# The head of a hybrid transformer block: modulation by blocks of 128 channels in TensorE column groups, against modulation by column halves

## The chip, the cores and the metric

The kernel runs on one core of a Trainium2 chip. The metric is the device time of one execution in microseconds (us), the median of several runs. Engines are named as in the profile: PE is TensorE's matmul side and PEld its weight loads, DVE is VectorE, ACT is ScalarE, POOL is GpSimd, and SP is SyncE, which here only issues DMA transfers (SPq is its row in the trace).

## The reference, cut to what matters

The kernel computes one layer of a trunk that carries a context stream `ctx` (256 tokens) and a latent stream `x` (1024 tokens) of 1024 channels through the same weights. The head is what the change is about:

```
mod   = silu(c)     @ w_mod + b_mod            # 1 x 6144
mod_c = silu(c_ctx) @ w_mod + b_mod
sh1, sc1, g1, sh2, sc2, g2 = split(mod, 6);  sh1c, sc1c, ... = split(mod_c, 6)
h  = x   * (1 + sc1)  + sh1
hc = ctx * (1 + sc1c) + sh1c
z    = h  @ w_in            # columns of four head groups: mLSTM, SGU, conv, S5
zc_d = hc @ w_in[:, OFF_D:] # the context goes into mLSTM and S5
...
x = layer_norm(ALPHA * x + g1 * (concat(y_a, y_b, y_c, y_d) @ w_out))
x = layer_norm(ALPHA * x + g2 * swiglu(x * (1 + sc2) + sh2))
```

The S5 group takes 256 columns of `z` for all 1280 tokens. Here they are computed as two products of 128 columns each, called block 0 and block 1 of the S5 input below.

## The kernel before, in words

Inputs of the large products are fp32 numbers split in a high and a low part (`hi`, `lo`), and a product is three passes: high by high, high by low, low by high (`PASSES`). `wload` fetches a weight tile of 512 KB into `raw`; `wsplit` makes its high part on ACT (L853, a CAST to `whl`) and its low part on DVE (L854). `projT` runs one such product with the channels as contraction, 8 steps `k` of 128 channels, into two PSUM banks of 512 latent tokens (L883) and one of 256 context tokens (L885). `projK` is the product with tokens as the output's partitions (L892).

A scheduler puts the instructions of the written program in an order for each engine, by data, by free buffers and by priority; each engine then runs its own list in that order and waits there by semaphores. So what the code writes first need not run first, but a queue is never overtaken once it is built. That holds for the list of SP too, whose transfers start in order.

The head, as it was written:

- `mod_load(cg)` fetches the part of `w_mod` that makes shift and scale, in two column groups `cg`: each is 4 pages of 1 MB (eight transfers of 512 KB), for 4 of the 8 channel blocks.
- `mod_cols(cg)` multiplies: `ccol` (both conditions after SiLU, 2 columns) is the stationary operand, 512 columns of `w_mod` stream by, for 8 steps `k` and two halves `j` (L820, 2 rows of output, fp32). Each of these 16 fp32 matmuls is two records in the trace. The two rows are copied out of PSUM (L824), turned into columns by 8 small transposes (L826), and with the bias added they go into `modc` (L830).
- `streams(ks)` applies scale and shift to four blocks of context (`vx`, L917) and latent (`xt`, `s5Yg`, `s5V`, `s5W`; L917 on DVE for odd blocks, L919 on ACT for even ones), casts to the high part on ACT (L920) and subtracts for the low part on DVE (L921).
- Then `projT` of S5 block 0 over the four channel blocks done; then the same again for column group 1. Block 1 comes later, in the loop over `b` behind the head, over all eight `k`.
- `s5_pre` and `s5_unit_tables` (on DVE, ACT and PE; lines L53 to L268) prepare the tables of the S5 recurrence; they depend on small parameters only and run between the other work.
- `zs` copies of ACT (L994) move the S5 input out of PSUM, a transfer writes it to `zd` in DRAM, and eight transfers for each block read it back as `s5U` with another layout. A table travels through DRAM in the same way: `s5TT` to `s5dr` to `s5M`. The units of the recurrence then start with PE's L287 on `s5U` and DVE's L292 on its result.

## Time and profile before

| | us |
|---|---|
| three runs before | 1180.8, 1176.69, 1179.63 |
| median | 1179.63 |
| the profiled execution, own time | 1178.48 |
| its span in the trace | 1176.70 |
| granted TensorE clock, mean | 0.986 |

The profiled execution is 1178.48 us by its own time, 1.78 us more than the span between its first and last record. Start times in the trace count from the span's start. A row of the timeline gives start, duration, engine, line of the kernel, operation, the tiles written and read, shape and the number of instructions put together in the row. Where a query puts several in a row, the duration is from the first's start to the last's end; matmuls overlap in it. A window row gives, for a stretch of time, its length, then the busy time of each engine with its instructions, the granted clock of TensorE (1.00 is full speed), the mean busy share of the 16 DMA engines and their rate in GB/s.

### The profile page before, as it was taken

The page shows a single profiled execution, that of the slowest core. Times are in us where ns is not written, and L with a number is a line of the kernel's source. Part 1 is how long each engine was busy: PE and PEld are TensorE (multiplying, and loading weights), DVE is VectorE, ACT ScalarE, POOL GpSimd, SP SyncE. Part 2 cuts the span into 40 slices and gives each one's busy share as a digit, 9 for nine tenths or more (in the row PEclk, how much of TensorE's full clock was granted, in tenths as well). Part 3 has the DMA queues.
Part 4 walks back from the last instruction along what each step waited for, and adds up shares of the span by engine and source line. Part 5 has one row for each costly group of instructions (what it writes and reads, how often), then busy time and mean ns, then how long its engine had stood idle before and what let it go on. Part 6 is the DMA issues. An engine that isn't in the chain of part 4 may idle for free.

```text
span 1176.7 us, 15244 instructions
## 1 busy us (share of the span) xinstructions
PE 1133.6 (96%) x5671; PEld 896.3 (76%) x5671; DVE 932.8 (79%) x1837; ACT 446.9 (38%) x691; POOL 9.6 (1%) x30
## 2 busy tenths in 40 slices
PE   6999999999999999989999999999999999999994
PEld 1487788667888778868887888888888878788883
DVE  6588999988899889879867667675767576777898
ACT  1454344422325433582233333233323243533433
POOL 0010000000000000000000000000000000000000
PEclk9999999999999999999999999999999989999997
DMA  9542111022143256352222233414342488856723
GB/s 362 208 128 88 45 48 49 35 68 72 54 143 109 90 170 207 106 217 84 96 106 102 80 125 125 139 44 141 107 143 82 134 291 281 290 197 212 268 70 143
DMA packets 57483, 160.57 MB, mean 136 GB/s; under 512 B 5377, under 2 KB 9633, under 8 KB 57026
## 3 DMA queue, kind: packets, MB, share of 16 engines
q1 hardware_dynamic: 56994, 158.62, 39.3%
q8 instruction: 44, 0.72, 0.2%
q0 software_dynamic: 272, 0.70, 0.2%
q10 hardware_dynamic: 144, 0.29, 0.1%
q14 instruction: 29, 0.24, 0.1%
HBM read 130.77 MB, written 28.82 MB: 136 GB/s over the span
## 4 chain that ended last, share of the span: by engine, by line
PE 77%; DVE 12%; DMA 7%; ACT 2%; issue 1%; POOL 0%; SPq 0%; DVEq 0%; ACTq 0%; POOLq 0%
PE mm L1344 16%; PE mm L883 13%; PE a L1344 8%; PE mm L1476 5%; PE mm L1183 5%; PE b L1344 4%; PE b L883 4%; PE a L1476 3%; PE b L1476 3%; PE mm L892 3%; DMA raw<-in_w_dram 2%; PE c L1476 2%; PE b L564 1%; DVE whl L854 1%; DMA whl<-gd 1%
## 5 line engine op out<-in xcount | busy, mean ns | idle before, releaser
L853 ACT CAST whl<-raw 128x512 fp32r<-128x512 f32 (+1 forms) x198 | 121.4, 622 | 278.6 <-PE mm L883 71.0
L883 PE MATMUL mm<-pg,whl 128*128 128x512 f32 x816 | 217.9, 406 | 1.4 <-ACT pg L1206 1.2
L1344 PE MATMUL mm<-pg,whl 128*128 128x512 f32 x864 | 204.8, 389 | 0.0
L1344 PEld LDWEIGHTS mm<-pg,whl 128*128 128x128 f32 x864 | 162.1, 188 | 33.8
L854 DVE TENSOR_TENSOR whl<-raw,whl 128x512 fp32r<-128x512 f32 (+1 forms) x198 | 135.5, 690 | 60.0 <-ACT whl L853 58.1
L883 PEld LDWEIGHTS mm<-pg,whl 128*128 128x128 f32 x816 | 147.6, 189 | 39.1 <-issue 7.0
L1344 PE MATMUL a<-pg,whl 128*128 128x512 f32 x432 | 104.2, 390 | 0.3 <-ACT whl L853 0.3
L1344 PEld LDWEIGHTS a<-pg,whl 128*128 128x128 f32 x432 | 80.9, 188 | 17.8 <-ACT whl L853 0.7
L1476 PE MATMUL mm<-pg,pg 128*128 128x512 f32 x315 | 88.2, 390 | 0.0
L853 ACT CAST pg<-raw 128x1024 fp32r<-128x1024 f32 (+1 forms) x46 | 45.7, 993 | 73.5 <-DVE raw L1455 38.7
L1476 PEld LDWEIGHTS mm<-pg,pg 128*128 128x128 f32 x315 | 59.0, 188 | 12.7 <-ACT pg L853 0.6
L854 DVE TENSOR_TENSOR pg<-raw,pg 128x1024 fp32r<-128x1024 f32 (+1 forms) x46 | 52.9, 1151 | 15.5 <-ACT pg L853 15.3
L892 PE MATMUL mm<-whl,pg 128*128 128x256 f32 (+1 forms) x448 | 63.1, 288 | 0.0
L892 PEld LDWEIGHTS mm<-whl,pg 128*128 128x128 f32 x448 | 58.1, 190 | 1.5 <-issue 1.1
L853 ACT CAST pg<-whl 128x1024 fp32r<-128x1024 f32 (+1 forms) x42 | 40.8, 976 | 38.8 <-DMA whl<-gd 19.3
L854 DVE TENSOR_TENSOR pg<-whl,pg 128x1024 fp32r<-128x1024 f32 (+1 forms) x42 | 47.3, 1131 | 8.3 <-ACT pg L853 8.1
L1344 PE MATMUL b<-pg,whl 128*128 128x512 f32 x216 | 51.9, 389 | 0.0
L1183 PE MATMUL mm<-whl,pg 128*128 128x512 f32 x192 | 50.2, 398 | 0.3 <-DVE pg L1171 0.3
L1183 PE MATMUL mm<-pg 128*128 128x512 f32 x192 | 49.4, 400 | 0.1
L1476 PE MATMUL a<-pg,pg 128*128 128x512 f32 x156 | 48.0, 389 | 0.0
L1476 PE MATMUL b<-pg,pg 128*128 128x512 f32 x156 | 48.0, 389 | 0.0
L1344 PEld LDWEIGHTS b<-pg,whl 128*128 128x128 f32 x216 | 40.5, 188 | 8.4
(473 smaller groups left out, 1796.9 us busy)
## 6 DMA issues: line engine op xcount, KB each, us to landing
raw<-in_w_dram SPq DMA_DIRECT2D x84, 512.0 KB
gd<-pg SPq DMA_DIRECT2D x22, 1024.0 KB
whl<-gd SPq DMA_DIRECT2D x35, 512.0 KB
pg<-in_wm_dram SPq DMA_DIRECT2D x16, 512.0 KB
raw<-in_wo_dram SPq DMA_DIRECT2D x16, 512.0 KB
raw<-in_wt_dram SPq DMA_DIRECT2D x14, 512.0 KB
mw<-in_w_mod_dram SPq DMA_DIRECT2D x24, 256.0 KB
vx<-in_w_mod_dram SPq DMA_DIRECT2D x24, 256.0 KB
```

What stands on the lines that cost most here:

```text
L564: pe.matmul(ps[:, x * 65:(x + 1) * 65], lhsT=D[d][:, x], rhs=vx[:, h, :], start=True, stop=True)
L853: a.copy(hi, r)
L854: v.tensor_tensor(lo, r, hi.bitcast(F32), op=SUB)
L883: pe.matmul(ps[h], lhsT=W(wi, k), rhs=rhs(hi, h, k), **f)
L892: pe.matmul(ps, lhsT=lhs(hi, k), rhs=Ws[k // 4](wi, k % 4), start=(k == 0 and n == 0), stop=(k == 7 and n == 2))
L1183: pe.matmul(ps, lhsT=Yr(hi, half, k)[:, t * 128:(t + 1) * 128], rhs=Ws[k // 2](wi, k % 2), start=(i + n == 0), stop=(i == 7 and n == 2))
L1344: pe.matmul(ps, lhsT=W[:, wi, k, :], rhs=B[b][hi][:, k], start=(first and k + n == 0), stop=(k == 3 and n == 2), skip_group_check=True)
L1476: pe.matmul(ps[t], lhsT=Ag[:, hi, k, t * 128:(t + 1) * 128], rhs=Bg[:, wi, k], start=(first and k0 + k + m == 0), stop=(k0 + k == NK - 1 a ...
```

## The change

Modulation and the first use of its result go by eight blocks of 128 channels.

- The host layout of `w_mod` is by block: `wm[k]` has, for one block, the 128 shift columns and the 128 scale columns over all 1024 contraction rows, 1 MB.
- `arrive(k)` fetches what block `k` needs: two halves of `wm[k]`, 512 KB of the latent, 128 KB of the context, and for the first two blocks the weight tile of S5 block `k`. The targets rotate in three (`s5Yg`, `vx`, and `s5h` with `s5V` for `wm`; three places of `xt` for the latent; `s5r1`, `s5r2`, `s5sc` for the context), so block `k+3` can be fetched once block `k` has been read.
- `modulate(k)` makes shift and scale of the block by 8 matmuls of 32 output rows and 256 columns (L903). The stationary operand `c32` has the two conditions in the first 2 of 32 columns and zeros in the others. Contraction steps `g` = 0 to 3 of a half go into four 32-row parts of one PSUM bank, which are four column groups of TensorE. One DVE copy takes 128x256 out of PSUM (L906), and two matmuls by a constant `quad` (L909) both sum the four parts and turn rows to columns. Two additions on DVE write `modc` (L911).
- The latent's scale is now on ACT for all blocks (L920), where odd blocks were on DVE.
- After `modulate(k)` the block goes through all three passes of both S5 products, into PSUM banks that both keep over the whole loop (`acc`); block 0 of the channels is used for S5 block 1 one step late. The `zs` copies of both S5 blocks stand behind channel block 7. `s5_pre` is written after the loop.

Line numbers in the head change: L820, L824, L826, L830 become L903, L906, L909, L911; L845, L853, L854 become L820, L828, L829; L883, L885, L892 become L858, L860, L867; L917, L919, L920, L921 become L918, L920, L921, L922. Behind the head a line of before is 8 lower, but L784 is L785.

```diff
-CST = (..., ("maskf", 128), ("maskb", 128))
+CST = (..., ("maskf", 128), ("maskb", 128), ("quad", 2))
...
-    g["wm"] = f(x["w_mod"][0][:, 0:2 * D].reshape(4, 2, 128, 2, 2, 512).transpose(4, 0, 2, 1, 3, 5))
+    g["wm"] = f(x["w_mod"][0][:, 0:2 * D].reshape(8, 128, 2, 8, 128).transpose(3, 1, 0, 2, 4))
...
+    c["quad"] = np.tile(np.eye(32, 2, dtype=np.float32), (4, 1))
...
-        def mod_cols(cg, ws, tags):
-        ...
-        def mod_load(cg):
-        ...
-        w0 = mod_load(0)
-        S = s5_pre(e, s5, A["s5p"])
-        ...
-        mod_cols(0, w0, "aa")
-        streams(range(4))
-        Wd[0] = wsplit(Wd[0])
-        zps = [projT(Wd[0], (0, 1), Hr, hcr, ks=range(4), last=False)]
-        mod_cols(1, w1_, "ac")
-        streams(range(4, 8))
+        c32 = s5.tile([128, 8, 32], F32, name="c32", tag="s5M", bufs=2)
+        v.memset(c32, 0.0)
+        v.tensor_copy(c32[:, :, 0:2], cs)
+        xs = mx.tile([128, 3, D], F32, name="xt", tag="ap")
+        cx, ws, Wd = {}, {}, []
+
+        def arrive(k):
+            if k % 3 == 2:
+                ws[k] = [s5.tile([128, 4, 256], F32, name="s5h"), s5.tile([128, 4, 256], F32, name="s5V", bufs=2)]
+            else:
+                w = mx.tile([128, 8, 256], F32, name="vx", tag="vx") if k % 3 else s5.tile([128, 8, 256], F32, name="s5Yg", tag="s5Yg")
+                ws[k] = [w[:, i * 4:i * 4 + 4] for i in range(2)]
+            for i in range(2):
+                ld(ws[k][i], A["wm"][k, :, i * 4:i * 4 + 4])
+            if k == 0:
+                ld(cst, A["cst"])
+            ld(xs[:, k % 3], A["xt"][:, k])
+            n = ("s5r1", "s5r2", "s5sc")[k % 3]
+            cx[k] = s5.tile([128, 256], F32, name=n, tag=n)
+            ld(cx[k], A["ct"][:, k])
+            if k < 2:
+                Wd.append(wload(wT["d"][k], 8, 128))
+
+        def modulate(k):
+            pm = e.ps("b")
+            for n in range(2):
+                for g in range(4):
+                    pe.matmul(pm[g * 32:(g + 1) * 32, 0:256], lhsT=c32[:, n * 4 + g, :], rhs=ws[k][n][:, g],
+                              start=(n == 0), stop=(n == 1))
+            mrow = e.tmp([128, 512], "hs")
+            v.tensor_copy(mrow[:, 0:256], pm[:, 0:256])
+            pt = e.ps("b")
+            for j in range(2):
+                pe.matmul(pt[:, j * 2:j * 2 + 2], lhsT=mrow[:, j * 128:(j + 1) * 128], rhs=cst[:, off["quad"]], start=True, stop=True)
+            for j in range(2):
+                v.scalar_tensor_tensor(mc[:, j, k], pt[:, j * 2:j * 2 + 2], float(j), bc(b1[:, j, k:k + 1], [128, 2]), op0=ADD, op1=ADD)
+            ...
+            for s_, x, hi, lo in ((0, xs[:, k % 3], H[0][k // 2][:, k % 2], H[1][k // 2][:, k % 2]),
+                                  (1, cx[k], hc[0][:, k], hc[1][:, k])):
+                if s_:
+                    v.tensor_scalar(x, x, modc[:, 8 + k, s_:s_ + 1], modc[:, k, s_:s_ + 1], op0=MUL, op1=ADD)
+                else:
+                    a.activation(x, x, AF.Identity, scale=modc[:, 8 + k, s_:s_ + 1], bias=modc[:, k, s_:s_ + 1])
+                a.copy(hi, x)
+                v.tensor_tensor(lo, x, hi.bitcast(F32), op=SUB)
+
+        acc = [(dict(enumerate(e.ps(t) for t in tags)), e.ps(c)) for tags, c in ((("mm", "mm"), "a"), (("mm", "a"), "c"))]
+        for k in range(8):
+            arrive(k)
+            modulate(k)
+            if k < 2:
+                Wd[k] = wsplit(Wd[k])
+                if k:
+                    projT(Wd[1], (0, 1), Hr, hcr, ks=(0,), acc=acc[1], last=False)
+            for b in range(min(k, 1) + 1):
+                projT(Wd[b], (0, 1), Hr, hcr, ks=(k,), acc=acc[b], first=(k == 0), last=(k == 7))
+        S = s5_pre(e, s5, A["s5p"])
...
         for b in range(2):
             zs = s5.tile([128, 8, 160], F32, name="s5zs", tag=("s5Yg", "s5V")[b], bufs=b + 1)
-            if b:
-                ps, cps = projT(wtile(wT["d"][1], 8, 128), (0, 1), Hr, hcr)
-            else:
-                ps, cps = projT(Wd[0], (0, 1), Hr, hcr, ks=range(4, 8), acc=zps[0], first=False)
+            ps, cps = acc[b]
```

How the instructions stand. PE, the start of the program before: modulation of a whole column group, and behind it products of S5 block 0 (`mm` and `a` are PSUM banks, `pg` pages with the latent's or `w_mod`'s data, `hs` the copied rows, `cst` the constants):

```order
L820 MATMUL a<-pg,ccol 2x512 x16
L826 MATMUL b<-cst,hs 128x2 x8
L820 MATMUL c<-pg,ccol 2x512 x5
L885 MATMUL a<-pg,whl 128x256
L885 MATMUL a<-yd,whl 128x256
L885 MATMUL a<-pg,whl 128x256 x2
```

PE now, from the end of the products of channel blocks 4 and 5 to the start of those of 6 and 7 (`c_86` is `c32`; `s5Yg` and `vx` hold `w_mod` of blocks 6 and 7):

```order
L858 MATMUL mm<-pg,whl 128x512
L858 MATMUL a<-pg,whl 128x512
L860 MATMUL c<-pg,whl 128x256
L903 MATMUL b<-s5Yg,c_86 32x256 x5
L909 MATMUL b<-cst,hs 128x2 x2
L903 MATMUL b<-vx,c_86 32x256 x8
L909 MATMUL b<-cst,hs 128x2 x2
L202 MATMUL b<-cst,s5S_595 128x128
L202 MATMUL b<-cst,s5S_596 128x128
L860 MATMUL a<-pg,whl 128x256
L860 MATMUL c<-pg,whl 128x256
```

The products of an even block and the odd one behind it now stand together behind both blocks' modulation; the same holds for blocks 2 and 3, and 4 and 5.

DVE before, around the first instruction of the recurrence (L292; `whl` low parts are L854, the L255 to L268 rows are tables):

```order
L268 TENSOR_TENSOR s5Es<-s5Es,s5ta 128x320
L255 TENSOR_SCALAR s5ta<-cst,s5hi_126 128x160 x2
L256 TENSOR_SCALAR s5ta<-s5ta 128x320
L259 SCALAR_TENSOR_TENSOR s5Es<-cst,s5hi_126,s5ta 128x160 x2
L260 SCALAR_TENSOR_TENSOR s5Es<-cst,s5lo_127,s5Es 128x160
L854 TENSOR_TENSOR whl<-raw,whl 128x512
L260 SCALAR_TENSOR_TENSOR s5Es<-cst,s5lo_127,s5Es 128x160
L292 TENSOR_TENSOR s5r_668<-b,s5Ec 128x320
```

DVE now, from the last low part of the latent and the context (`pg`, `yd`) to the first L292:

```order
L922 TENSOR_TENSOR pg<-xt,pg 128x1024
L922 TENSOR_TENSOR yd<-s5r_449,pg 128x256
L196 TENSOR_TENSOR s5tc<-s5pi,s5Bb 128x256
L197 TENSOR_TENSOR s5S_622<-s5S_622,s5tc 128x256
L192 TENSOR_TENSOR s5tc<-s5pi,s5Bb 128x256
L268 TENSOR_TENSOR s5Es<-s5Es,s5ta 128x320
L210 TENSOR_TENSOR s5ta<-s5pr,s5par 128x288
L829 TENSOR_TENSOR whl<-raw,whl 128x512 x2
L222 COPY s5BD<-s5Bb 64x8x16
L223 COPY s5BD<-s5Bb 64x8x16
L239 TENSOR_TENSOR s5TT<-s5TT,b 32x2x16
L240 TENSOR_TENSOR s5TT<-s5TT,s5dd 32x2x16
```

Behind these stand four more L829 of 544 columns (weight tiles of the mLSTM's values) ahead of L292; before, those four stood behind it.

SP before, in the same place (`zd` is the S5 input in DRAM, `s5U` its rereading, `raw` the next weight tiles):

```order
L784 DMA zd<-s5zs 128x1280
L845 DMA raw<-in_wv_dram 128x1088
L784 DMA s5U<-zd 128x1x160 x4
L784 DMA s5dr<-s5TT 32x480
L784 DMA s5U<-zd 128x1x160 x4
L784 DMA s5M<-s5dr 128x1x128 x4
L784 DMA zd<-s5zs 128x1280
```

SP now, from the last block's context to the same transfers:

```order
L895 DMA s5r_449<-in_ct_dram 128x256
L820 DMA raw<-in_wk_dram 128x1024 x2
L960 DMA mw<-in_w_mod_dram 128x512
L820 DMA raw<-in_wv_dram 128x1088 x2
L785 DMA s5dr<-s5TT 32x480
L785 DMA zd<-s5zs 128x1280
L785 DMA s5M<-s5dr 128x1x128 x4
L785 DMA s5U<-zd 128x1x160 x8
L785 DMA zd<-s5zs 128x1280
```

The transfers of `s5M` now stand ahead of all `s5U`, and the write of `zd` behind that of `s5dr`.

More of the change, by code (lines that the diff above doesn't have):

```diff
@@ L711 @@
 CST = (("ident", 128), ("jrow", 160), ("dl16", 16), ("dl4", 4), ("rst", 104),
-       ("sel1", 10), ("sel2", 40), ("maskf", 128), ("maskb", 128))
+       ("sel1", 10), ("sel2", 40), ("maskf", 128), ("maskb", 128), ("quad", 2))
 VEC = (("b1", "b_mod", 0, 16), ("b2", "b_mod", 16, 24), ("mnw", "mlstm_norm_w", 0, 2), ("glw", "sgu_ln_w", 0, 2),
@@ L905, in body @@
-        x4 = [s5.tile([128, D], F32, name="s5V", tag="s5V", bufs=2) for _ in range(2)]
-        for i in range(2):
-            ld(x4[i], A["xt"][:, 4 + i])
-        x4.append(s5.tile([128, D], F32, name="s5W", tag="s5W"))
-        ld(xt[0][:, 2], A["xt"][:, 6])
-        ld(x4[2], A["xt"][:, 7])
-        xr = lambda k: (xt[0][:, 0], xt[0][:, 1], xt[1][:, 0], xt[1][:, 1], x4[0], x4[1], xt[0][:, 2], x4[2])[k]
         hc = [page([128, 8, 256], F32R), mx.tile([128, 8, 256], F32R, name="yd", tag="yd")]
@@ L913, in body @@
         H = [[None] * 4 for _ in range(2)]
-        def split_mod(x, hi, lo, s, b, on_dve):
-            if on_dve:
-                v.tensor_scalar(x, x, s, b, op0=MUL, op1=ADD)
-            else:
-                a.activation(x, x, AF.Identity, scale=s, bias=b)
-            a.copy(hi, x)
-            v.tensor_tensor(lo, x, hi.bitcast(F32), op=SUB)
-        def streams(ks):
-            for k in ks:
-                split_mod(cx[:, k], hc[0][:, k], hc[1][:, k], modc[:, 8 + k, 1:2], modc[:, k, 1:2], True)
-            for k in ks:
-                if k % 2 == 0:
-                    for hl in range(2):
-                        H[hl][k // 2] = page([128, 2, D], F32R)
-                split_mod(xr(k), H[0][k // 2][:, k % 2], H[1][k // 2][:, k % 2], modc[:, 8 + k, 0:1], modc[:, k, 0:1], k % 2)
@@ new lines, in modulate @@
+        def modulate(k):
[11 more added lines that the diff above has]
+                v.scalar_tensor_tensor(mc[:, j, k], pt[:, j * 2:j * 2 + 2], float(j), bc(b1[:, j, k:k + 1], [128, 2]), op0=ADD, op1=ADD)
+            if k % 2 == 0:
+                for hl in range(2):
+                    H[hl][k // 2] = page([128, 2, D], F32R)
+            for s_, x, hi, lo in ((0, xs[:, k % 3], H[0][k // 2][:, k % 2], H[1][k // 2][:, k % 2]),
[6 more added lines that the diff above has]
+                v.tensor_tensor(lo, x, hi.bitcast(F32), op=SUB)
```

30 lines of the change are left out of this document (removed).

## The prediction

> **What bounds the kernel now.** I read the page's busy shares and slices first, then windows over the head, then the timeline at the window borders, then groups of rows for durations.
>
> ```profile
> PE 1133.6 (96%) x5671; PEld 896.3 (76%) x5671; DVE 932.8 (79%) x1837; ACT 446.9 (38%) x691; POOL 9.6 (1%) x30
> ...
> PE   6999999999999999989999999999999999999994
> ```
>
> PE is busy 96% of the span, and 43 us are left in which it is not; the first slice (29 us) holds a good part. So there are two ways to gain: less PE work where PE is the bound, or a shorter head. The windows:
>
> ```profile
> core 0: us, PE busy (x) PEld busy (x) DVE busy (x) ACT busy (x) POOL busy (x), PEclk, DMA share, GB/s
> 0.00:5.60 5.60, 0.00 (x0) 0.00 (x0) 0.82 (x7) 1.50 (x2) 1.78 (x9) 1.00 0.68 188
> 5.60:28.10 22.50, 16.89 (x40) 3.71 (x40) 18.10 (x98) 1.11 (x3) 0.00 (x0) 0.97 1.01 402
> 28.10:35.25 7.15, 7.15 (x12) 1.04 (x11) 7.00 (x15) 5.39 (x9) 0.00 (x0) 0.61 1.03 415
> 35.25:42.70 7.45, 7.45 (x32) 4.10 (x32) 3.32 (x4) 3.14 (x4) 0.00 (x0) 1.00 1.03 406
> 42.70:55.00 12.30, 12.30 (x43) 4.78 (x41) 2.57 (x4) 2.33 (x4) 0.00 (x0) 1.00 0.14 53
> 0.00:80.88 80.88, 69.67 (x274) 34.60 (x275) 54.23 (x183) 29.47 (x50) 5.20 (x19) 0.96 0.62 234
> 80.88:240.00 159.12, 156.30 (x971) 120.91 (x970) 151.35 (x427) 73.26 (x142) 3.83 (x10) 1.00 0.19 61
> 0.00:80.88 80.88, 33.26 (x64) 5.36 (x64) 0.96 0.62 234
> ```
>
> From 5.6 to 42.7 us DMA is full at 402 to 415 GB/s. Behind that PE is full up to the recurrence, which starts on DVE at 80.88. From there to 240 PE (156.30) and DVE (151.35 of 159.12) are both nearly full. The last row is L820 alone: modulation takes 33.26 us of PE, 64 records.
>
> **The change, part by part.**
>
> PE, modulation.
>
> ```profile
> 28.10 7.22 PE L820 MATMUL c<-pg,ccol 128*2 128x512 f32 x10
> 40.77 4.45 PE L820 MATMUL a<-pg,ccol 128*2 128x512 f32 x10
> 71.67 1.28 PE L231 MATMUL b<-s5V,s5BD 128*32 128x128 f32 x10
> 78.37 1.36 PE L287 MATMUL b<-s5U,s5W 128*64 128x160 f32 x16
> ```
>
> A warm record of 512 columns takes 0.43 us (4.45/10, the last one's tail included), one at low clock 0.72. The new one streams 256 columns, so 0.215, and a block has 8 matmuls of 2 records: 16 x 0.215 = 3.44 us one after another, or 0.86 if four column groups run side by side; eight blocks 27.5 or 6.9. No row shows four groups. The nearest is L287, whose 64-row outputs alternate between two groups: with 0.30 for the last, (1.36 - 0.30)/15 = 0.071 us per record of 160 columns. L231 in one group takes (1.28 - 0.28)/9 = 0.111 for 128, which is 0.139 for 160. Two groups give 1.96 times, nearly full overlap, so I take 0.86 and keep 3.44 for the first rival. The removed L820 work is thus 27.5 warm us, and 6.9 replace it.
>
> The Trainium skill, "TensorE: Matmul & The Clock Gate", Part 3, "Measured speedup vs the span model", gives 2.38 times for three column tiles, less than three. At 0.79 of each tile's share a block would take an estimated 1.09 us instead of 0.86, and the forecast would be up to 1.8 us later; the trace here shows only the two-group pair of rows above, which overlap better.
>
> S5 products. These are unchanged in amount, 96 L883 and 48 L885 before, but all now stand in the loop.
>
> ```profile
> 60.36 3.18 PE L883 MATMUL mm<-pg,whl 128*128 128x512 f32 x13
> 63.38 0.28 PE L885 MATMUL a<-pg,whl 128*128 128x256 f32 x1
> 63.49 0.40 PE L883 MATMUL mm<-pg,whl 128*128 128x512 f32 x1
> 78.17 0.28 PE L885 MATMUL a<-pg,whl 128*128 128x256 f32 x1
> ```
>
> By starts, L883 takes (63.38 - 60.36)/13 = 0.232 and L885 0.11, so one pass of one S5 block over one channel block is 0.58, and a pair of channel blocks (2 x 2 x 3 passes) 7.0 us. The last row is the end of block 1 now, 78.45.
>
> DVE. The rows that price it:
>
> ```profile
> 8.71 0.20 DVE L1041 TENSOR_SCALAR wc<-wc 128x62 f32<-128x62 f32 x1 [3.92 <-DMA wc<-in_conv_t_dram]
> 20.34 0.25 DVE L141 RECIPROCAL s5U<-s5U 128x16 f32<-128x16 f32 x1
> L854 DVE TENSOR_TENSOR whl<-raw,whl 128x512 fp32r<-128x512 f32 x8 | 5.3, 686 | 3.0 <-ACT whl L853 2.9
> L921 DVE TENSOR_TENSOR pg<-xt,pg 128x1024 fp32r<-128x1024 f32 x3 | 3.6, 1218 | 0.0
> L921 DVE TENSOR_TENSOR yd<-vx,pg 128x256 fp32r<-128x256 f32 x8 | 2.8, 417 | 0.0
> L824 DVE COPY hs<-a 2x512 f32<-2x512 f32 x2 | 1.4, 678 | 7.4 <-PE a L820 7.4
> L830 DVE SCALAR_TENSOR_TENSOR modc<-b,cols 128x8 f32<-128x8 f32 x4 | 0.5, 161 | 2.4 <-PE b L826 2.4
> L917 DVE TENSOR_SCALAR s5Yg<-s5Yg,modc 128x1024 f32<-128x1024 f32 x1 | 0.8, 815 | 0.9 <-DMA s5Yg<-in_xt_dram 0.9
> L268 DVE TENSOR_TENSOR s5Es<-s5Es,s5ta 128x320 f32<-128x320 f32 x1 | 0.5, 492 | 2.1 <-ACT s5ta L267 2.1
> ```
>
> - Gone: two L824 (1.4), four L830 (0.5), four latent scales of 1024 (4 x 0.815 = 3.2).
> - New: eight copies of 256 columns, priced 0.41 each by the 256-wide L921 (3.3; between 0.2, half of L824's width and time, and 0.68); 16 additions of 0.16 (2.6); a copy for `c32` (0.4).
> - Moved ahead of L292: four L829 (4 x 0.686 = 2.7) and one L268 (0.5).
>
> 54.2 - 5.1 + 6.3 + 3.2 = 58.6 us. The `c32` copy stands behind L1041's wait, so DVE starts in earnest at 8.71; with 0.8 of the work before 5.6 (first window), an idle-free L292 is at 8.7 + 57.8 = 66.5 at best. Behind the last low part the order has six L829 (4.1), L268 (0.5), four tables of 256 to 288 columns (1.6) and four small rows (0.4): the last low part is at 59.9 or later. Four passes of the pair need it or the one before (4 x 0.58 = 2.3), so the S5 products end at 62.2 or later. `c32`'s zeroing lies in DVE's idle time before 4.0 us and costs nothing; that cover is long.
>
> DMA. Head bytes are the same 14 MB at about 405 GB/s, last landing near 42 us, and 7 us of products from there: no end before 50. It is not what sets the end. The `quad` column adds 1 KB. New are waits on SP: `arrive(k+3)` waits for block `k`'s matmuls and its last low part, and everything behind it in SP's list waits too, the mLSTM's weight tiles and the S5 transfers. Two blocks are 3.3 MB, 8.1 us at 405 GB/s, under the period of a pair below (11.7), so I cost these waits at nothing; if slots come free late, the next late thing is a pair's `xt`.
>
> Walk through the loop. The second channel block's low parts stand in DVE's order behind L141, which now starts at 20.34. Ahead of it come two blocks' copies (0.8), additions (0.6) and context scales (0.8), two latent and two context low parts (2.4 and 0.8), four L829 (2.7) and `c32` (0.4): 8.5 us, so they end at 20.6 + 8.5 = 29.1. Four passes behind them (2.3) and semaphores: 32 us for blocks 0 and 1. From there the order shows pairs: PE can't start 2, 3 before block 3's `quad`. Modulation's last matmuls wait for `w_mod` in a slot that the pair before has read and for the PE queue; then comes a serial chain:
>
> ```profile
> L919 ACT ACTIVATE xt<-xt,modc 128x1024 f32<-128x1024 f32 x2 | 2.5, 1241 | 6.3 <-DVE modc L830 6.3
> L920 ACT CAST pg<-xt 128x1024 fp32r<-128x1024 f32 x3 | 3.0, 1045 | 0.0
> L853 ACT CAST whl<-raw 128x512 fp32r<-128x512 f32 x8 | 4.7, 616 | 11.6 <-PE mm L883 8.4 <-DMA raw<-in_wt_dram 3.3
> L994 ACT COPY s5zs<-mm 128x512 f32<-128x512 f32 x4 | 2.4, 593 | 0.9 <-PE mm L883 0.9
> ```
>
> Matmuls' tail about 1.0, copy 0.41, two `quad` matmuls 0.45, additions 0.25, scale 1.24, cast 1.05, some 0.3 between engines: 4.7 us with PE without products. A pair's period is 7.0 + 4.7 = 11.7, and the S5 products end (call it T) at 32 + 3 x 11.7 = 67.1; the DVE bound was 62.2. The odd latent scales moved to ACT are in that chain; ACT has only 29.5 us of work in the 80.88, so beside it they cost nothing.
>
> From T to L292.
>
> ```profile
> 67.97 0.33 SPq L784 DMA_DIRECT2D zd<-s5zs  x1
> 71.50 2.81 SPq L784 DMA_DIRECT2D s5U<-zd  x4
> 74.62 0.35 SPq L784 DMA_DIRECT2D s5dr<-s5TT  x1
> 77.58 2.44 SPq L784 DMA_DIRECT2D s5M<-s5dr  x4
> 80.88 0.49 DVE L292 TENSOR_TENSOR s5r<-b,s5Ec 128x320 f32<-128x320 f32 x1
> ```
>
> Now the write of S5 block 0 (67.97) goes out, and its rereading 3.53 later, while PE is still on block 1. In the changed order everything waits for T. On ACT stand casts of 0.62 (two) and `zs` copies (three of about 0.5) and two small rows for the table; one part runs before T, which leaves 3.6; DVE's two small rows 0.3. On SP, `s5dr` goes first, at T + 3.9; `s5M` waits behind it 2.96 (74.62 to 77.58) and takes 2.44 to issue; only then come `s5U`, two issues (0.7 to the second's start) and its landing, taken as the 2.96 of `s5dr`: T + 13.0. L292 comes at 80.1, 0.8 earlier than now. The `zd` write is covered by the wait for `s5dr`.
>
> The recurrence stage. Four L829 are gone from it, 2.7 us of DVE; and PE, which in the new order has nothing of the S5 input left from T to L292, can take up to 13 us of the mLSTM products there, out of this stage. With DVE at 151.35 of 159.12 I take DVE as the bound and its 7.8 us of idle as staying: -2.7. Behind 240 us the program is the same.
>
> Sum: -0.8 - 2.7 = -3.5 us on 1178.5, which is 1175.0. The profiled execution lies 1.15 below the median of 1179.6, and I sum against the profiled one. No difference means within 0.3%, 3.5 us.
>
> **The rivals.**
>
> R1, column groups don't overlap: each block costs 3.44 instead of 0.86, 2.58 more, eight times 20.6. T 87.7, L292 100.7, +19.8 - 2.7: 1195.6. Against it speak the L287 rows.
>
> R2, PE's lead is kept: PE's products end at 67.1 instead of 78.45, and if PE fills the wait for `s5U` with mLSTM products the whole stage ends earlier. The cap is DVE: 151.35 - 2.7 leaves 148.6 of 159.12, so at most 10.5, with the 0.8 11.3: 1167. For it: PE's 156.30 of 159.12 is the tighter of the two now. Against: DVE's waits have stayed at 7.8 us for each 159. I put it at 1162 to 1168.
>
> R3, the slower side: PE waits between pairs, and runs at half clock behind each wait. The 28.10 to 35.25 window has a clock of 0.61 after PE had waited for data; at half clock for x us, 7.15 - x/2 = 0.61 x 7.15, x = 5.6. If three pairs do this, 3 x 2.8 = 8.4, with half of one for the first pair 1.4: T 76.9, L292 89.9, +9.0 - 2.7: 1184.8. It decides from T = 70.6 (no gain) and 74.1 (slower by over 0.3%). Against it: modulation matmuls fall into the waits and keep PE partly busy.
>
> The Trainium skill, "TensorE: Matmul & The Clock Gate", "HAM oscillation", says that a PE gap of over about 3.4 us brings the clock back to half; that speaks against this change, since the chain of 4.7 us is about such a gap, and by it the sum would be R3's. By that rule the trace agrees so far as the 0.61 goes; which of the new gaps reaches it, no run here shows yet.
>
> **How the numbers follow.** Main case 0.50, 1171 to 1179; R1 0.08; R2 0.17; R3 0.25, 1180 to 1190. The range 1163 to 1190 leaves out R1 and the edges of R2 and R3, under 2 in 10. Faster by over 0.3% (below the median less 3.5, 1176.1): R2's 0.17 and rather more than half of the main case, 0.28: 0.45. Same: the rest of the main case 0.22 and 0.06 of R3. Slower: 0.19 of R3 and R1's 0.08.
>
> **What would show it.** Right: 16 L903 records of a block in about 0.9 us; pairs of products with waits of 4 to 5 us between; products ending at 65 to 69; first L292 at 78 to 82; DVE nearly full behind it with the same idle. Wrong: L903 at 3 us or more per block (R1); granted clock below 0.9 in the windows of the loop (R3); DVE idle in the stage behind L292 falling below 5 us (R2). What would upset all of it is a DVE order that stalls on L829 behind late `raw` transfers, or `arrive` waiting for its slots.

## The result, and the profile after

The changed kernel takes 1186.08 us (median of 6 runs, 1184.22 to 1191.82), against 1179.6 for the kernel before on the same chip: a ratio of 1.0064, 95% interval 1.0041 to 1.0088. It is 6.5 us slower where 3.5 us faster was forecast. The profiled execution took 1186.95 with a span of 1185.2 us, so the two profiled executions differ by 8.5. This difference is what the accounts below add up to.

The page's busy line and PE slices after the change:

```profile
PE 1126.6 (95%) x5751; PEld 906.7 (77%) x5751; DVE 933.0 (79%) x1853; ACT 455.3 (38%) x697; POOL 9.9 (1%) x30
...
PE   3999999999999999989999999999999999999994
```

PE has 7.0 us less work than before (1133.6), and still the span is longer. What grew is time in which PE does nothing: from the start to the last matmul it rose from 26.3 to 41.9 us (all PE records of each trace laid over each other). Seven less and 15.6 more is 8.6, the profiled difference. The first slice fell from 6 to 3 tenths.

Windows over the head, before and then after, in the columns of the prediction's windows:

```profile
0.00:43.00 43.00, 31.79 (x82) 8.93 (x83) 29.25 (x123) 11.43 (x18) 1.78 (x9) 0.92 0.97 376
43.00:80.00 37.00, 37.00 (x186) 24.79 (x184) 24.09 (x58) 18.03 (x33) 3.42 (x10) 1.00 0.22 72
```

```profile
5.60:28.00 22.40, 10.06 (x49) 5.38 (x49) 15.04 (x78) 5.57 (x9) 0.00 (x0) 1.00 0.98 364
28.00:35.00 7.00, 6.70 (x23) 5.56 (x24) 6.81 (x27) 2.02 (x4) 0.00 (x0) 1.00 0.49 158
35.00:42.00 7.00, 5.89 (x52) 3.93 (x51) 4.10 (x16) 3.53 (x4) 0.00 (x0) 0.86 0.44 152
42.00:55.00 13.00, 12.07 (x68) 7.82 (x67) 8.48 (x21) 2.44 (x4) 0.00 (x0) 0.81 0.65 205
0.00:43.00 43.00, 23.65 (x124) 15.73 (x125) 28.05 (x129) 13.62 (x20) 1.78 (x9) 0.96 0.75 265
43.00:80.00 37.00, 34.18 (x214) 24.78 (x213) 27.16 (x71) 20.56 (x39) 3.30 (x10) 0.95 0.50 164
```

In the first 43 us PE is busy 8 us less, and the DMA share falls from 0.97 to 0.75: the last block of `latent` is issued at 58.27 only, behind slots that PE reads later than before. From 43 to 80, where PE was full (37.00 of 37.00), it now is not.

The start and the loop, from PE's timeline after (start, length, line, what ended the idle time in brackets):

```profile
10.59 1.93 PE L903 MATMUL b<-s5Yg,c 128*32 128x256 f32 x16 [10.59 <-DVE c L878]
18.22 1.22 PE L858 MATMUL mm<-pg,whl 128*128 128x512 f32 x2 [3.19 <-ACT whl L828]
...
22.71 1.94 PE L903 MATMUL b<-vx,c 128*32 128x256 f32 x16
...
35.74 0.28 PE L860 MATMUL c<-pg,whl 128*128 128x256 f32 x1
...
37.57 0.61 PE L909 MATMUL b<-cst,hs 128*128 128x2 f32 x4 [0.55 <-DVE hs L906]
...
42.19 1.48 PE L858 MATMUL mm<-pg,whl 128*128 128x512 f32 x3
...
51.19 0.28 PE L860 MATMUL c<-pg,whl 128*128 128x256 f32 x1
...
56.99 0.86 PE L858 MATMUL mm<-pg,whl 128*128 128x512 f32 x3
...
63.88 0.28 PE L860 MATMUL c<-pg,whl 128*128 128x256 f32 x1
66.19 1.07 PE L903 MATMUL b<-vx,c 128*32 128x256 f32 x16
...
76.45 0.28 PE L860 MATMUL c<-pg,whl 128*128 128x256 f32 x1
```

The four L860 rows end the passes of blocks 0 and 1, 2 and 3, 4 and 5, 6 and 7: the last ends at T = 76.7, and the pairs take 15.4, 12.7 and 12.6 us. A block's 16 L903 records take 1.07 us at 66.19, but 1.93 in blocks 0 and 1. At 42.19 three L858 take 1.48 us, and 0.86 at 56.99. A narrow window (66.19 to 66.22) shows the first four of the 16 running together:

```profile
66.19 0.42 PE L903 MATMUL b<-vx,c 128*32 128x256 f32 x4
```

The first row waits for DVE's copy into `c32`. DVE's and SP's own timelines show why, and what comes after T:

```profile
9.64 0.20 DVE L1033 TENSOR_SCALAR wc<-wc 128x62 f32<-128x62 f32 x1 [5.07 <-DMA wc<-in_conv_t_dram]
10.37 0.17 DVE L878 COPY c<-ccol 128x16 f32<-128x16 f32 x1
...
89.34 0.49 DVE L292 TENSOR_TENSOR s5r<-b,s5Ec 128x320 f32<-128x320 f32 x1 [3.11 <-PE b L287]
```

```profile
80.34 0.34 SPq L785 DMA_DIRECT2D s5dr<-s5TT  x1
82.63 2.61 SPq L785 DMA_DIRECT2D s5M<-s5dr  x4
85.34 4.92 SPq L785 DMA_DIRECT2D s5U<-zd  x8
```

From T the chain over `s5dr`, `s5M` and `s5U` takes 12.6 us to L292 at 89.34 (80.88 before). The waits of PE, grouped, in the first 100 us (us in total, times, longest):

```profile
PE b L903 <- DVE c L878: 10.6, 1, 10.6
PE mm L858 <- ACT whl L828: 6.4, 3, 3.2
PE b L909 <- DVE hs L906: 5.3, 8, 1.5
```

The last row is PE's idle time ahead of the `quad` matmuls, 5.3 us for all eight blocks, 1.5 of them in the first. The stretch without products that was forecast at 4.7 us a pair takes 4.2 to 4.4 us (51.47 to 55.62, for one). PE is idle in 1.1 us of each, and modulation and `quad` fill the rest.

### The profile page after: what moved, and what is told of

It is laid out like the page before. It is cut to its first block, busy times and chain, and to the rows that moved or that the text cites. A ratio compares the mean times of both kernels' runs of the same rounds, so it can differ in the third digit from the quotient of the medians.

```text
span 1185.2 us, 15456 instructions
## 1 busy us (share of the span) xinstructions
PE 1126.6 (95%) x5751; PEld 906.7 (77%) x5751; DVE 933.0 (79%) x1853; ACT 455.3 (38%) x697; POOL 9.9 (1%) x30
## 4 chain that ended last, share of the span: by engine, by line
PE 64%; DMA 7%; DVE 6%; ACT 1%; issue 1%; DVEq 0%; SPq 0%; ACTq 0%
PE mm L1336 16%; PE mm L858 8%; PE a L1336 8%; PE mm L1175 6%; PE mm L1468 5%; PE b L1336 4%; PE b L858 4%; DMA raw<-in_w_dram 4%; PE b L1468 3%; PE a L1468 3%; PE c L1468 2%; DMA whl<-in_w_dram 1%; PE b L564 1%; PE mm L867 1%; DMA mw<-in_w_mod_dram 1%
## 5 line engine op out<-in xcount | busy, mean ns | idle before, releaser
L858 PE MATMUL mm<-pg,whl 128*128 128x512 f32 x792 | 217.5, 412 | 8.1 <-ACT whl L828 6.4
L828 ACT CAST whl<-raw 128x512 fp32r<-128x512 f32 (+1 forms) x198 | 121.5, 622 | 264.2 <-PE mm L858 66.7
L829 DVE TENSOR_TENSOR whl<-raw,whl 128x512 fp32r<-128x512 f32 (+1 forms) x198 | 135.4, 691 | 58.3 <-ACT whl L828 56.5
L858 PEld LDWEIGHTS mm<-pg,whl 128*128 128x128 f32 x792 | 146.7, 193 | 42.7 <-ACT whl L828 6.8
L828 ACT CAST pg<-raw 128x1024 fp32r<-128x1024 f32 (+1 forms) x46 | 45.7, 994 | 76.0 <-DVE raw L1447 39.4
L829 DVE TENSOR_TENSOR pg<-raw,pg 128x1024 fp32r<-128x1024 f32 (+1 forms) x46 | 52.9, 1152 | 16.2 <-ACT pg L828 16.1
L867 PE MATMUL mm<-whl,pg 128*128 128x256 f32 (+1 forms) x448 | 64.9, 292 | 0.5 <-DVE whl L829 0.3
L867 PEld LDWEIGHTS mm<-whl,pg 128*128 128x128 f32 x448 | 58.8, 192 | 3.8 <-issue 2.2
L828 ACT CAST pg<-whl 128x1024 fp32r<-128x1024 f32 (+1 forms) x42 | 40.8, 977 | 34.5 <-DMA whl<-gd 17.3
L829 DVE TENSOR_TENSOR pg<-whl,pg 128x1024 fp32r<-128x1024 f32 (+1 forms) x42 | 47.4, 1132 | 7.3 <-ACT pg L828 7.3
```

Of the source, the lines that this page charges most:

```text
L828: a.copy(hi, r)
L829: v.tensor_tensor(lo, r, hi.bitcast(F32), op=SUB)
L858: pe.matmul(ps[h], lhsT=W(wi, k), rhs=rhs(hi, h, k), **f)
L867: pe.matmul(ps, lhsT=lhs(hi, k), rhs=Ws[k // 4](wi, k % 4), start=(k == 0 and n == 0), stop=(k == 7 and n == 2))
```

## The experiments

Fourteen kernels ran. Ratios are to the kernel before on the same chip. Where two of these kernels are compared, it is by their ratios and intervals.

**pipe: products two blocks behind the modulation.** In the changed kernel PE's order has block `k`'s products right behind its modulation. Here they stand behind that of block `k+2`.

```
-            for b in range(min(k, 1) + 1):
-                projT(Wd[b], ..., ks=(k,), acc=acc[b], ...)
+            if k > 1:
+                for b in range(2):
+                    projT(Wd[b], ..., ks=(k - 2,), acc=acc[b], ...)
+        for k in (6, 7):
+            for b in range(2):
+                projT(Wd[b], ..., ks=(k,), acc=acc[b], ...)
```

> Products of channel block k are written behind the modulation of block k+2, so that the next block's modulation stands among products on PE and no pair of blocks waits for a whole modulation chain. Theory A (the serial modulation chain of 4 to 5 us that PE waits out before each pair, and the transfers of the S5 input that all wait for the last product): S5 products end at 63 to 67 us instead of 76.6, first L292 at 76 to 80, total 9 to 12 us under the changed kernel, about 1175. Theory B (half TensorE clock behind the waits is what costs): only the slow records of the first two pairs are saved, some 5.5 us, products end at 71, total about 1180.5. Theory C (column groups or DVE's own load set the time): no change, 1186.

1185.86 us, 1.0040 [1.0014, 1.0065], not told apart from the changed kernel. Yet L292 comes at 78.52, 10.8 us earlier than in the changed kernel and 2.4 earlier than before:

```profile
78.52 0.48 DVE L292 TENSOR_TENSOR s5r<-b,s5Ec 128x320 f32<-128x320 f32 x1
```

The window behind it shows where the lead went:

```profile
81.00:100.00 19.00, 11.35 (x69) 9.50 (x67) 13.34 (x42) 2.71 (x5) 0.00 (x0) 0.66 0.52 156
```

PE works 11.35 of 19 us, at a clock of 0.66; its longest wait, 5.0 us, is for L828's cast of the mLSTM value weights, which SP issues at 87.26:

```profile
PE mm L867 <- ACT whl L828: 5.0, 1, 5.0
```

So the start of the recurrence, on which the whole forecast was summed, does not set the time by itself.

**late2: only S5 block 0 in the loop.** Block 1's products stand behind the loop, with weights fetched as before.

```
-            if k < 2:
+            if k < 1:
...
-            for b in range(min(k, 1) + 1):
-                projT(Wd[b], ..., ks=(k,), acc=acc[b], ...)
+            projT(Wd[0], ..., ks=(k,), acc=acc[0], ...)
...
+            if b:
+                projT(wtile(wT["d"][1], 8, 128), (0, 1), Hr, hcr, acc=acc[1])
```

> Only S5 block 0 is taken in the loop over channel blocks; block 1 is done behind it over all eight, with its weights fetched there, as before the change. Modulation by blocks in column groups stays. Theory A: block 0 is complete at 60 to 64 us (DVE's work sets it), its way through DRAM (13 us) is covered by block 1's 14 us of products, first L292 at 74 to 78, total about 1174. Theory B: the clock is no better with less work per block, gain under 4 us, 1182 or more. Theory C: 1186.

1193.93 us, 1.0107 [1.0085, 1.0130], as slow as the changed kernel or slower. With less product work between the small matmuls the clock is lower, by two windows:

```profile
28.00:35.00 7.00, 6.71 (x26) 3.16 (x25) 3.34 (x16) 1.00 (x1) 0.00 (x0) 0.50 0.74 245
35.00:42.00 7.00, 6.42 (x29) 3.28 (x29) 4.79 (x17) 1.48 (x3) 0.00 (x0) 0.61 0.36 107
```

L292 comes at 90.42: taking one S5 block out of the loop did not bring the recurrence forward.

**serial: one column group instead of four.**

```
-                    pe.matmul(pm[g * 32:(g + 1) * 32, 0:256], ...
-                              start=(n == 0), stop=(n == 1))
+                    pe.matmul(pm[0:32, 0:256], ...
+                              start=(n + g == 0), stop=(n * 4 + g == 7))
...
```

> All eight matmuls of a block's modulation go into the same 32 output rows (one column group) and quad sums 32 rows instead of 128. If four groups run side by side as the 1.06 us per block in the trace says, a block costs 3.44 + tail, about 2.6 us more, and with two blocks in series ahead of each pair the head is 15 to 20 us longer: 1201 to 1206. If the column groups bring nothing (theory C): same as the changed kernel, 1186.

1205.86 us, 1.0204 [1.0179, 1.0229]. The window for L903 alone, in the changed kernel and in this one (PE busy, PEld busy, clock, DMA share, GB/s):

```profile
0.00:100.00 100.00, 11.96 (x128) 3.97 (x128) 0.97 0.64 217
```

```profile
0.00:100.00 100.00, 34.95 (x128) 12.72 (x128) 0.98 0.56 193
```

Four groups do the same 128 records in 11.96 us instead of 34.95. That is 2.9 times as fast with the last records' ends counted in; from start to start it is nearly four times, 0.22 us for one record here and for four together in the changed kernel. The overlap that the change relies on is real, and its price without overlap (20.6 us in R1; measured 1.0204 - 1.0064 = 1.4%, 16.5 us) was about right. Against the kernel before, whose modulation takes 33.26 us of PE, this kernel is 24 us slower: that is about what the order by blocks costs without the column groups.

**warm2: more work for PE.** Six matmuls of 256 columns, which nobody reads, behind the modulation of blocks 1 and 3.

```
+            if k in (1, 3):
+                fill = e.ps("b")
+                for i in range(6):
+                    pe.matmul(fill[:, 0:256], lhsT=e.ident, rhs=mrow[:, 0:256], start=(i == 0), stop=(i == 5))
```

> Six extra matmuls of 256 columns on the modulation's copied rows, behind the modulation of blocks 1 and 3, into a PSUM tile that nobody reads; they fill the wait of PE for ACT's scale and cast. Theory B: the product records of the first two pairs take 0.23 instead of 0.43 us, products end 4 to 5 us earlier (72), total about 1181.5. Theory A: the waits remain, and the clock is worth at most what the extra matmuls take, 0 to 3 us: 1183 to 1186.

1183.23 us, 1.0026 [1.0008, 1.0043]: the interval just touches the changed kernel's. The window where that had 0.86 is at full clock, and L292 comes at 84.40:

```profile
35.00:42.00 7.00, 6.45 (x46) 5.16 (x46) 6.14 (x19) 4.87 (x6) 0.00 (x0) 1.00 0.55 156
```

So the low clock in the loop seems to have a cost, and at most a part of the 8.5 us.

**bhalf: the kernel before with half its modulation.** Only the odd contraction steps are multiplied, 32 records instead of 64; all transfers stay.

```
-            for k in range(8):
+            for k in range(1, 8, 2):
```

> The kernel before with half of its modulation matmuls left out (only the odd contraction steps, 32 of 64 records, so shift and scale are wrong; all transfers stay). Theory D (PE's work and its waits add up to the time, and the modulation stood in time in which PE would wait for transfers anyway): of some 16 us of matmuls less, most comes back as waiting in the first 43 us, and the time falls by 0 to 6 us, 1175 to 1181. Theory E (each us of modulation taken from PE is a us of time): 12 to 16 us less, 1165 to 1169.

1178.51 us, 0.9986 [0.9969, 1.0003]. The page, and the window of the first 43 us:

```profile
PE 1123.8 (96%) x5639; PEld 896.3 (76%) x5639; DVE 932.2 (79%) x1837; ACT 449.4 (38%) x693; POOL 9.5 (1%) x30
```

```profile
0.00:43.00 43.00, 26.40 (x77) 8.01 (x77) 29.02 (x124) 11.85 (x18) 1.79 (x9) 0.88 0.97 375
```

PE has 9.8 us less to do and L292 comes at 71.71, 9.2 us earlier; yet the runs show no clear difference, and the interval allows a gain of 3.7 us at most. Up to the last matmul PE's idle time rises from 26.3 to 35.1. Some of that is in the first 43 us (16.6 instead of 11.2), where PE stands in front of a full DMA queue (0.97 in both): work removed there becomes waiting for data. But a lead of 9.2 us does reach L292 and is lost behind it. From 351 us on, in the time of the kernel before, PE's records are the same in both, by line and tile. There the lead is still 4.8 us, and at the last matmul 1.0. Of the 3.8 us lost in this common part, 3.4 are clock: 17.1 us at half clock against 10.2.

**early2: the start of the changed kernel without its wait.** The copy on ACT, the transfer of `wc` on SP's queue instead of POOL's.

```
-        v.tensor_copy(c32[:, :, 0:2], cs)
+        a.copy(c32[:, :, 0:2], cs)
...
-        gp.dma_start(wc, A["conv_t"])
+        ld(wc, A["conv_t"])
```

> The changed kernel with two moves at the start: the stationary operand c32 is copied on ACT instead of DVE, and the convolution weights wc come through SP's queue late, so that DVE no longer waits for them at 9.6 us. Theory D: PE's first matmul is at 6 instead of 10.6 us and the first two blocks are 3 to 5 us earlier, PE waits that much less: 1181 to 1183. Theory F (the first S5 unit's start sets the time and the later blocks' transfers set that): no change, 1186.

1187.09 us, 1.0056 [1.0031, 1.0080]. The first L903 starts at 6.13 instead of 10.59 and T comes at 72.8, 3.9 earlier; L292 is at 88.58, only 0.8 earlier. On SP the weight tiles of the next products (`in_wt`) stand behind the sixteen `s5U` reads, and their cast on ACT waits 7.8 us, PE for that cast 3.0:

```profile
94.93 9.10 SPq L820 DMA_DIRECT2D raw<-in_wt_dram  x4
100.29 2.41 ACT L828 CAST whl<-raw 128x512 fp32r<-128x512 f32 x4 [7.82 <-DMA raw<-in_wt_dram]
```

**pipek and best3: the late weights brought forward.** `pipek` is `pipe` with the mLSTM's context key and value products written ahead of the `s5U` reads, `best3` that with the two edits of `early2`.

```
+        Wk = [wtile(A["wk"][kh], 4, 256) for kh in range(2)]
+        ...
+        Wv = wvg()
+        ...
```

> The kernel pipe (modulation of the next blocks among products) with the second half of the mLSTM value weights fetched ahead of the S5 input's rereading, by writing the context's key and value products ahead of it. In pipe PE waited 5.0 us at about 85 us for that weight tile's cast. Theory D: that wait goes, 4 to 5 us less than pipe, about 1181; first L292 at about 79 as in pipe. Theory F: pipe has its first L292 2.4 us ahead of the kernel before and is still 4 us slower, so its start isn't the bound; if it were, nothing would change here, 1186.

> All three together: products behind the modulation of block k+2, value weights ahead of the S5 input's rereading, c32 on ACT and wc late. Theory D: PE's waits of the head fall by 4 + 5 us against pipe: 1176 to 1178. If the waits only move to the next late tile: 1182 to 1186.

`pipek`: 1185.41 us, 1.0037 [1.0020, 1.0054]; the wait of 5.0 is gone, and L292 is at 85.29. `best3`: 1182.85, 1.0011 [0.9990, 1.0031], level with the kernel before and faster than the changed one. Its window at 81 to 100 still shows PE at 14.39 of 19 and a clock of 0.73:

```profile
81.00:100.00 19.00, 14.39 (x84) 10.69 (x82) 14.88 (x45) 2.65 (x5) 0.00 (x0) 0.73 0.52 160
```

ACT's timeline and PE's waits in that window:

```profile
91.85 2.39 ACT L828 CAST whl<-raw 128x512 fp32r<-128x512 f32 x4 [9.86 <-DMA raw<-in_wt_dram]
PE a L317 <- DVE s5S L309: 2.9, 2, 1.7
PE mm L858 <- ACT whl L828: 0.7, 1, 0.7
```

The long wait for weights is now ACT's, for the next tiles; PE waits 0.7 us for their cast, and longer, 2.9 us, for DVE's L309 in the recurrence.

**best5 and best7: the reads on another queue, and work for the clock.** `best5` is `best3` with twelve of the sixteen reads issued by POOL; `best7` adds eight matmuls on a constant tile ahead of block 0 and six unread ones behind the modulation of blocks 0 and 1.

```
-                e.dma(Ub[:, g], ...)
+                (e.dma if b * 8 + g < 4 else gp.dma_start)(Ub[:, g], ...)
```

> The kernel best3 with twelve of the sixteen rereads of the S5 input issued by POOL instead of SP. In best3 the next weight tiles (raw from in_wt) stand on SP behind fifteen such rereads until 86.8 us, ACT waits 9.9 us for them and PE is idle or at low clock from 81 to 92. Theory D (the time is PE's work and its waits): the weight tile comes 5 to 7 us earlier, PE's waits and slow records at 81 to 92 fall by 3 to 5 us, total 1178 to 1180. If the recurrence on DVE is what holds PE there: no change against best3, 1183.

> best5 with matmuls that nobody reads, eight on a constant tile ahead of the first block's modulation and six on the copied rows behind the modulation of blocks 0 and 1, so that TensorE is at full clock when the first products start. Theory D with the clock as part of PE's work: the S5 products lose their slow records of the first two blocks, 3 to 6 us of PE less, and with the early start 1174 to 1177. If the clock isn't held by them, or the waits for data set the first blocks: as best5.

1185.73 us, 1.0043 [1.0022, 1.0063], and 1184.09, 1.0033 [1.0012, 1.0054]. Neither gains on `best3`, whose PE waited little for those weights. `best7` has the fewest idle us of PE up to 80 of all kernels here, 6.8 (before 11.2), and is not faster for it.

**beforeg: the same two transfer edits on the kernel before.** (`wc` on SP, twelve reads on POOL.)

> The kernel before, with the same two moves of transfers alone: twelve of sixteen rereads of the S5 input on POOL, and wc late through SP. Theory D: PE waits only 0.8 us between 80 and 100 us there, and its first 43 us are paced by transfers, so nothing is gained: within 2 us of the kernel before, 1179 to 1182. If these moves are worth something by themselves, it shows here too: 1176 or less.

1177.21 us, 0.9976 [0.9960, 0.9992]: faster than both kernels. L292 comes at 76.7, and PE is idle 9.3 us up to 80 instead of 11.2. Why the reads on POOL go with a gain here and with none in `best5` stays open; the two edits were not run apart.

**bdrop: less PE work far behind the head.** The kernel before, with one of three passes left out of four products, 64 records.

```
+                    if n == skip:
+                        continue
...
-            ps, _ = projT(wtile(wT["ca"][j], 8, 128), (0, 1), Hr)
+            ps, _ = projT(wtile(wT["ca"][j], 8, 128), (0, 1), Hr, skip=1)
```

> The kernel before with one of three passes (high by low) left out of the four conv products, 64 matmuls of 512 columns between about 90 and 165 us, 64 x 0.232 = 14.8 us of PE; all transfers, splits and DVE work stay (the conv branch is less exact). It is the counterpart of bhalf, which took 9.8 us of PE work out of the first 43 us. Theory D (behind the head PE's work is the bound): 12 to 15 us less, 1165 to 1169. Theory G (from 80 to 240 us DVE is the bound, as the prediction took it): 0 to 5 us less, 1175 to 1181.

1183.53 us, 1.0038 [1.0010, 1.0065]: slower, with less to do. The page and two windows:

```profile
PE 1131.5 (95%) x5607; PEld 894.6 (75%) x5607; DVE 930.4 (78%) x1837; ACT 454.9 (38%) x697; POOL 10.0 (1%) x30
```

```profile
160.00:180.00 20.00, 17.14 (x122) 15.50 (x123) 18.34 (x62) 3.86 (x9) 0.00 (x0) 0.83 0.00 1
365.00:385.00 20.00, 16.22 (x80) 12.94 (x82) 14.26 (x45) 8.25 (x11) 0.00 (x0) 0.69 0.12 50
```

The 64 records are 64 x 0.232 = 14.8 us of work; PE's busy time falls by 2.1 and its idle time rises by 12.7. (This execution took 1188.97 us, 5.4 above the median.) In the first window, right behind the cut products, DVE is the fuller engine (18.34 of 20) and the clock is 0.83; in the second, 200 us later, 0.69.

**bgroups: the column groups alone, in the kernel before.** Modulation by halves of the channels as before, into four groups.

```
-                    pe.matmul(pm[j][0:2], lhsT=cs[:, k, :], rhs=..., start=(k == 0), stop=(k == 7))
+                    g = (k + 2 * j) % 4
+                    pe.matmul(pm[j][g * 32:(g + 1) * 32], lhsT=c32[:, k, :], rhs=..., start=(k < 4), stop=(k > 3))
...
-                    pe.transpose(ps[...], mrow[0:2, x * 128:(x + 1) * 128], e.ident[0:2, 0:2])
+                    pe.matmul(ps[...], lhsT=mrow[:, x * 128:(x + 1) * 128], rhs=cst[:, off["quad"]], ...)
```

> One half of the change alone: the kernel before with its transfers, column halves and order, but each half's modulation in four column groups (stationary operand padded to 32 columns, sums and turning by quad). Theory D (modulation's PE time in the first 43 us only covered waits for transfers): PE busy falls by 15 to 20 us, its waits rise by as much, time within 3 us of the kernel before, 1176 to 1182. Theory E (PE time saved in the head is time saved): 1160 to 1168. Theory H (waits also bring the low clock, and the products behind them pay): 2 to 6 us slower than before.

1178.99 us, 0.9996 [0.9980, 1.0012]. The page, the window of the first 43 us, and modulation (L822) alone:

```profile
PE 1127.6 (96%) x5687; PEld 901.6 (76%) x5687; DVE 932.7 (79%) x1838; ACT 450.3 (38%) x694; POOL 9.4 (1%) x30
```

```profile
0.00:43.00 43.00, 27.79 (x114) 10.93 (x114) 27.57 (x123) 10.13 (x18) 1.78 (x9) 0.88 0.97 375
```

```profile
0.00:100.00 100.00, 18.53 (x64) 2.66 (x64) 0.90 0.61 223
```

Modulation falls from 33.26 to 18.53 us and PE's whole work by 6.0, nearly the 7.0 of the changed kernel, and the time does not move. The saved 14.7 us went two ways up to 80 us: PE idles 17.3 us instead of 11.2, and its clock is at half for 20.5 us instead of 6.8, so that the products take longer. In the old order, then, the column groups neither gain nor lose; in the order by blocks they are worth 16.5 us (`serial`). The changed kernel's interval lies wholly above this one's, so what made it slower is the other half of the change, the order by blocks.

**best8: the order by blocks at its best here.** `best3` with the six unread matmuls behind the modulation of blocks 0 and 1 (`warm2`'s edit with `if k < 2:`).

> best3 with six matmuls that nobody reads behind the modulation of blocks 0 and 1, which held the clock in warm2. Theory H: the first blocks' products run at full clock, 2 to 4 us less than best3, 1179 to 1181, level with the kernel before. If the clock is lost elsewhere by then: as best3, 1183.

1179.19 us, 1.0000 [0.9985, 1.0015]: the order by blocks, mended, is level with the kernel before, and faster than the changed kernel. Its windows in the loop are at full clock, where the changed kernel has 0.86 and 0.81 from 35 on:

```profile
28.00:35.00 7.00, 7.00 (x47) 4.97 (x47) 5.95 (x26) 2.58 (x4) 0.00 (x0) 1.00 0.79 280
35.00:42.00 7.00, 6.38 (x43) 4.19 (x41) 5.64 (x18) 3.25 (x4) 0.00 (x0) 1.00 0.86 270
42.00:55.00 13.00, 11.73 (x79) 7.44 (x77) 10.56 (x30) 5.74 (x9) 0.00 (x0) 1.00 0.76 243
```

`best3`'s interval overlaps this one, so the unread matmuls by themselves are not shown to gain.

**The marks side by side**, from the profiled executions: L292, then the stage from there to the end of the S5 output (its last L346), then the rest to the last record.

```
          L292    stage   rest    last record
before    80.88   143.6   948.9   1173.5
after     89.34   144.7   948.0   1182.0
bhalf     71.71   146.6   954.2   1172.4
bgroups   78.63   144.5   953.4   1176.5
pipe      78.52   147.2   955.2   1181.0
pipek     85.29   139.6   958.5   1183.4
best3     82.34   141.2   953.2   1176.7
best8     81.00   139.2   951.3   1171.5
late2     90.42   144.1   954.6   1189.1
serial    97.86   145.0   958.4   1201.3
```

These are single executions (`best8`'s is the fastest of its ten, `pipek`'s the slowest), so a difference of a few us between two rows need not be one of the kernels.

Between before and after the numbers add up as if the late L292 were the cause (+8.5 +1.1 -1.0, before rounding). That they agree is chance. From 352.6 us of the kernel before (357.0 of the changed one) PE's records are the same by line and tile, and there the changed kernel is 4.4 us behind. It is 6.1 behind at 497, 9.0 at 523 and 8.6 at the last matmul. The step at 500 to 525 is a spell at half clock that the other execution does not have (before, then after):

```profile
500.00:525.00 25.00, 21.91 (x111) 16.07 (x110) 19.61 (x25) 21.85 (x32) 0.00 (x0) 1.00 0.69 255
500.00:525.00 25.00, 22.13 (x102) 16.98 (x101) 20.40 (x32) 18.47 (x26) 0.00 (x0) 0.86 0.83 292
```

The other rows of the table show the same: what is gained at L292 comes back in the two later columns, most plainly in `pipe` against the changed kernel (-10.8, then +2.5 and +7.2).

The granted clock of every execution is on record, and (1 - clock) x span says how much of it a kernel lost. It is a rough measure: it counts low clock in PE's idle time too, and the record of the clock starts some us into an execution. Medians over all executions, in us, beside the kernel before on the same chip (for the changed kernel beside the one profiled execution):

```
          lost    before   ratio of times
changed   17.8    16.5     1.0064
bhalf     19.4    16.5     0.9986
bgroups   20.0    15.3     0.9996
bdrop     23.0    15.3     1.0038
beforeg   14.1    15.9     0.9976
pipe      21.9    16.5     1.0040
late2     22.1    16.5     1.0107
serial    21.1    16.5     1.0204
warm2     15.9    16.5     1.0026
early2    21.3    16.5     1.0056
pipek     20.1    16.5     1.0037
best3     20.1    16.5     1.0011
best5     17.8    15.9     1.0043
best7     20.1    15.9     1.0033
best8     16.5    15.3     1.0000
```

The three kernels with PE work taken out of the kernel before (`bhalf`, `bgroups`, `bdrop`) lose 2.9 to 7.7 us more to the clock than it does. `pipe` has its L292 early and loses 5.4 more. Of the three with unread matmuls two lose least of all by blocks (`warm2`, `best8`), and `best7` does not. That a saving on PE is in part paid back in clock is thus seen over all executions, not in one trace alone.

## Why the prediction was wrong

The measured time lies in the stated range, but with the wrong sign. The term of the sum that failed is T, the end of the S5 products: 67.1 was forecast and 76.7 came, and so L292 at 89.34 instead of 80.1. With 89.34 in its place the sum gives 1178.5 + 8.5 - 2.7 = 1184.3, slower than before. A second step failed behind it: that a time at L292 is a time at the end. Step by step:

- **Column groups**: right. By starts, as 0.86 was counted, a block's 16 records take 0.9 us: four start within 0.02 us, and the next four 0.22 later. The 1.07 is from the first start to the last end. So the overlap is nearly full, and the lower one behind the 1.09 that was worked out from the Trainium skill, "TensorE: Matmul & The Clock Gate", Part 3, "Measured speedup vs the span model", does not show here. `serial` confirms the price of the rival R1.
- **Blocks 0 and 1 done at 32**: wrong, 36.0. The wait behind `wc` was seen (8.71 for DVE), but not that PE's first matmul waits for it too: it moves from 5.6 to 10.59. PE then has 10.06 us of work from 5.6 to 28, waits for the first casts, and runs its small matmuls at half speed.
- **The pair's period of 11.7**: wrong, 15.4, 12.7 and 12.6. The chain in it was nearly right as a stretch without products (4.2 to 4.4 us where 4.7 was taken), but PE is idle in only 1.1 us of it, 0.55 at a time. A group of four `quad` records takes 0.61 us, where 0.45 was taken. The mis-sized part is the products: from the first to the last of a pair 8.3 to 8.5 us instead of 7.0, with records of the next modulation and short waits among them, and 11.1 in the pair with the low clock. SP's waits for slots, put at nothing, cost PE nothing here: in the three pairs it waits for no transfer.
- **T at 67.1**: wrong by 9.6 (76.7), by the two steps above: 4.0 at blocks 0 and 1, 5.6 in the three pairs.
- **T to L292, 13.0**: right, 12.6, by the row of `s5M` and `s5U` on SP.
- **-2.7 in the stage, since DVE is the bound there**: wrong. The stage takes 144.7 us to the last L346, not less than the 143.6 before, and the window that matches the prediction's reads:

```profile
89.34:248.20 158.86, 152.85 (x921) 117.00 (x918) 148.31 (x418) 67.75 (x129) 4.30 (x10) 0.99 0.19 61
```

  DVE's work fell by 3.0 us and its idle time rose by 2.8, where I had let it stay at 7.8. Nor is "the program behind 240 us the same": by line and tile PE's list is that of before only from 352.6 us on.
- **The sum**: it went from the time of L292, as if all behind it moved along. `bhalf` and `pipe` move it by 9.2 and 2.4 us ahead of the old place without a gain that the runs show. And it gave the 20.6 us of saved modulation to the time through T. `bgroups` shows what becomes of such a saving in the old order: waits for the loads and low clock. In the profiled pair: modulation -21.6, `quad` matmuls against the old transposes +4.3, S5 products and those behind them on the same lines +5.8, other lines +4.4, idle +15.6.

R3 named the half clock and landed on the numbers (T 76.9, L292 89.9, 1184.8), but by a mechanism that is half wrong, so that its numbers are in part luck. Its low windows are there (0.86 and 0.81 from 35 to 55), but in one pair of the three, and not behind idle stretches of 4.7 us, since PE's waits there are 0.55; the late start, which it did not have, filled the rest. Of the "HAM oscillation" rule of the Trainium skill ("TensorE: Matmul & The Clock Gate") the trace bears out that PE falls to half speed in a loop with gaps, not that it takes a gap of 3.4 us: the spell from 40.4 on follows L903 and L909 records with a gap of 0.55.

**What is shown, and what is open.** Shown: in the old order the column groups do not change the time; the order by blocks makes it longer, and the column groups win back 16.5 us of that; the start of the recurrence does not set the time by itself; and the changed kernel's loss vanishes when the products run behind the modulation, the start is early and the weights ahead (`best3`, `best8`). Not shown: which single one of these pieces is the cause. `pipe`, `early2` and `pipek` each leave the kernel slower, with intervals that overlap the changed one's. Argued only: that the late start and the low clock cost time which PE, 95% busy, can't make up later. Open: why a shorter head or less PE work lowers the clock later in the program. Executions of one kernel lie up to 13 us apart, so a piece worth 2 us can't be told from none here.
